# Other kinds for the late taps of a convolution, and another form for some VectorE products

## The chip, the cores and the metric

The kernel runs on one core of one Trainium2 chip. The core has TensorE for matmuls (PE in the profile, its weight loads are PEld), VectorE (DVE), ScalarE (ACT), GpSimd (POOL) and SyncE (SP), and 16 DMA engines that all queues share. Each engine works through its own instructions in the order of the program; semaphores hold an instruction until what it needs is done. The metric is the time of one execution on the device in microseconds (us), the median over several executions. Before the change it is 2298.85 us, from three runs between 2296.11 and 2299.28.

## The reference

A two-layer encoder works on a residual stream of 1024 positions by 1024 columns in float32. In each layer an attention with eight heads and a depthwise convolution run side by side on the same projection, and their joined outputs go through one matrix; then follows a gated feed-forward part. What matters here, cut from the reference:

```python
for l in range(DEPTH):
    h = _rmsnorm(x, g_mix[l])
    p = h @ w_in[l]
    ...                                                # q_nope, q_rope, k_nope, k_rope, v from p
    y_attn = _mla_attention(q_nope, q_rope, k_nope, k_rope, v)
    a, gt = jnp.split(p[..., o3:], 2, axis=-1)
    u = a * jax.nn.sigmoid(gt)
    u = _dwconv(u, w_dw_conv[l], b_dw_conv[l])         # 31 taps per channel, 512 channels
    u = jax.nn.silu(_layernorm(u, g_conv_ln[l], b_conv_ln[l]))
    x = x + jnp.concatenate([y_attn, u], axis=-1) @ w_o[l]
    ...                                                # gated feed-forward part
```

A tap of the convolution multiplies a shifted copy of `u` by one weight per channel and adds it to the sum. 31 taps on four tiles of 128 channels by 1024 positions make 124 products and additions for each layer.

## The kernel before

Every layer is projection, attention, output matrix and feed-forward part, one after the other on TensorE. Values for matmuls are split into a high and a low part (`hi` and `lo`, float32 rounded to TensorE's format and what is left), and a product is three matmuls: high by high, high by low, low by high.

**Attention** runs over 64 steps in a layer, 8 heads times 8 blocks of 128 queries. A step n issues, in program order for every engine: the product of probabilities and values for an earlier block (`values`, L1532, tile `o`), the transposes of the probabilities (`turn`, L1509, tile `t`, split by ACT at L1511 and VectorE at L1512), the scores of step n+2 (`scores`, L1480), the exponentials of step n+1 (`expo`, L1490 on ACT), and then whatever hangs in `agenda[n]`. Work beside attention is placed by this agenda: an entry sets the place in each engine's instruction order, not a time.

**What hangs in the agenda.** A finished half of a head's output is copied by ACT (L1537) and completed by VectorE (L1538) into `yt`; two heads share one `yt`. POOL multiplies pairs of heads by the reciprocal sums (L1558), ACT and POOL split them into `ys` high and low (L198, L200). For the next to last head the product is done by VectorE in two halves (L1556), in steps 60 and 61. In step 55 POOL issues the first four DMAs of the output matrix `wo`, which cast while they load (L836); from step 58 on ACT writes the negative of each arrived, rounded part into a second tile (L179), and a DMA from POOL adds the weight itself there (L180), which leaves the low part. In steps 60 to 62 POOL adds up the four convolution tiles (L1701), for the norm over channels.

**The taps.** The nearest 56 taps of the 124 are done by VectorE while TensorE projects (L1673, one fused multiply and add). Some more are done there by ACT and a DMA that adds. What is left, 50 taps in layer 0 and 48 in layer 1, are the late taps: the function `tap_late` (L1682 on) does each in one of three kinds, with its product in a tile `late` of its own:

- `act`: ACT multiplies in two halves (L1687), and a DMA issued by POOL adds the product to the sum (L1695, accumulating).
- `pool`: POOL multiplies (L1690), the same kind of DMA adds.
- `both`: POOL multiplies (L1690) and POOL adds (L1693).

The accumulating DMAs stand in POOL's queue. Before it adds to a tile of the sum, an addition of either sort waits for the addition before it to the same tile; the taps go round the four tiles (`conv` 0 to 3), which have different numbers of late taps left, and the last few all belong to `conv` 3. Which kind a tap has, and in which step it stands, is set by

```python
kinds = [LATE_KINDS[2 * i // len(late)][i % 5] for i in range(len(late))]
costs, taken = [LATE_COST[kind] for kind in kinds], set()
for i, (j, t) in enumerate(late):
    n, steps = int(SIDE_TIME * sum(costs[:i]) / sum(costs)), self.tap_late(l, j, t, u[j], conv[j], kinds[i])
```

so the first half of the taps follows the first tuple of `LATE_KINDS`, the second half the other, five in turn; and the 56 steps of `SIDE_TIME` are shared out in proportion to `LATE_COST` (1.1 for `act`, 3.5 for `pool`, 4.8 for `both`). A change of kind therefore moves the other taps too.

The tiles named here (`late`, `yt`, `rb`, `ys`, `conv`) come from one set of 31 equal buffers of 128 by 1024 floats; a new tile takes over a free buffer and waits for the last reader of the old one.

**Ahead of attention** VectorE subtracts the rounded parts of the queries from the queries: `query_rope` at L694 twice in a layer, `query` at L709 four times.

Of the kernel before, what the change touches and what calls it, by code (L numbers as in the profile page):

```python
# [9 lines left out]
F32 = mybir.dt.float32  # L10
F32R = mybir.dt.float32r
I32 = mybir.dt.int32
AF = mybir.ActivationFunctionType
ALU = mybir.AluOpType
# [48 lines left out]
LAST_MULT = (60, 61)  # L63
# [2 lines left out]
ROW_AT = {0: (6,), 1: (7,)}  # L66
E = mybir.EngineType
MANUAL = [E.PE, E.DVE, E.Activation, E.Pool]
LATE_KINDS = (("pool", "both", "act", "pool", "act"), ("both", "pool", "both", "pool", "both"))
LATE_COST = {"act": 1.1, "pool": 3.5, "both": 4.8}  # L70
NEAR_TAPS = (12, 14, 16, 14)
NEAR_ORDER = (0, 1, 2, 3)
# [43 lines left out]
class Encoder:  # L116
# [398 lines left out]
    def project(self, l, carry):  # L515
        nc, a = self.nc, self.a
# [160 lines left out]
        def query_rope(i):  # L677
            p = ps[f"u{i}"]
            c, s = self.blk(f"rc{l}_{i}"), self.blk(f"rs{l}_{i}")
            nc.vector.tensor_tensor(out=c, in0=p, in1=st["cos"], op=ALU.mult)  # L680
            nc.vector.tensor_tensor(out=s, in0=p, in1=st["sin"], op=ALU.mult)
            st["rope", i] = c, s
            yield 2.44, 0.0
            if i == 0:
                return
            (c1, s1), (c2, s2) = st.pop(("rope", 0)), st.pop(("rope", 1))
            nc.vector.tensor_tensor(out=c1, in0=c1, in1=s2, op=ALU.subtract)
            nc.vector.tensor_tensor(out=c2, in0=c2, in1=s1, op=ALU.add)
            his = [self.blk(f"qr{l}_{i}", F32R) for i in range(2)]
            for hi, o in zip(his, (c1, c2)):  # L690
                nc.scalar.copy(out=hi, in_=o)
            yield 2.5, 1.0
            for i, (hi, o) in enumerate(zip(his, (c1, c2))):
                nc.vector.tensor_tensor(out=o.bitcast(F32R), in0=o, in1=hi.bitcast(F32), op=ALU.subtract)  # L694
                sp = hi, o.bitcast(F32R)
                yield 1.25, 0.0
                for p in range(2):
                    for h in range(DIRECT):
                        self.move(heads[h][0][p][NOPE + i * HALF:NOPE + (i + 1) * HALF, :],
                                  sp[p][h * HALF:(h + 1) * HALF, :])  # L700
                spills.extend((qrd[p][i].rearrange("h d t -> (h d) t"), sp[p]) for p in range(2))

        def query(j):
            n = self.blk(f"qn{l}_{j}")
            nc.vector.tensor_tensor(out=n, in0=ps[f"n{j}"], in1=st["rq"], op=ALU.mult)
            hi = self.blk(f"qns{l}_{j}", F32R)
            nc.scalar.copy(out=hi, in_=n)
            yield 1.22, 1.5
            nc.vector.tensor_tensor(out=n.bitcast(F32R), in0=n, in1=hi.bitcast(F32), op=ALU.subtract)  # L709
            sp = hi, n.bitcast(F32R)  # L710
            for p in range(2):
                for e in range(DIRECT if j == 0 else 0):
                    self.move(heads[e][0][p][0:NOPE, :], sp[p][e * 64:(e + 1) * 64, :])
                spills.append((qd[p][2 * j:2 * j + 2].rearrange("h d t -> (h d) t"), sp[p]))
            while j and spills:
                self.move(*spills.pop(0))
            yield 1.25, 0.0
# [56 lines left out]
        for i in range(2):  # L774
            held = lambda: launch(query_rope(0), len(seq) - 6)
            add(f"u{i}", "u2", ranked("u2", i, QL, f"u{i}", cqs), lambda i=i: query_rope(1) if i else iter(()), held if i else norm)
        for j in range(4):
            add(f"n{j}", f"u{j // 2}", ranked(f"u{j // 2}", j % 2, QL, f"n{j}", cqs), lambda j=j: query(j))
# [670 lines left out]
    def attention(self, l, u, conv, away, spill, kvs, loaded, ahead, wo, begun):  # L1449
        nc = self.nc  # L1450
# [66 lines left out]
        def values(group, c, n):  # L1517
            h, gg = divmod(group, 2)
            st = state[h]
            e = h % 2  # L1520
            main, aux = slice(e * 64, e * 64 + 64), slice(64 - e * 64, 128 - e * 64)
            if c == 0:
                if gg == 0 and e == 0:
                    st["y"], st["rb"] = self.blk(f"yt{l}_{h}"), self.blk(f"rb{l}_{h}")
                elif gg == 0:
                    st["y"], st["rb"] = state[h - 1]["y"], state[h - 1]["rb"]
                st["po"] = self.bank(f"o{l}_{h}_{gg}")
            y, rb, po = st["y"], st["rb"], st["po"]
            pt = st["pt"].pop((c, gg))
            for s in range(2):  # L1530
                for i in range(2):
                    nc.tensor.matmul(po, v[2 * c + i][:, h // 2, e, :], pt[s][:, i, :],  # L1532
                                     start=(c == 0 and i == 0 and s == 0), stop=(c == 3 and i == 1 and s == 1))
            if c < 3:
                return
            qs = HALVES[gg]
            nc.scalar.copy(out=y[main, qs], in_=po[aux, :])  # L1537
            nc.vector.tensor_tensor(out=y[main, qs], in0=po[main, :], in1=y[main, qs], op=ALU.add)  # L1538
            if h < HEADS - 2 and gg:
                agenda[n + 1].append(lambda: sums(h, main, st, y, rb))  # L1540
            elif h == HEADS - 1:
                if gg:
                    divide(y[main, qs], main, gg)
                else:
                    agenda[n + 1].append(lambda: (divide(y[main, qs], main, gg), finish(last, y, 0)))

        def sums(h, main, st, y, rb):
            pr = self.bank(f"sr{l}_{h}", (8, 128))
            nc.tensor.transpose(pr, st["sums"], self.ident)
            rs = self.cp.tile([8, 128], F32, name=f"rs{l}_{h}", tag="rs", bufs=2)  # L1550
            nc.vector.reciprocal(out=rs, in_=pr)
            nc.sync.dma_start(out=sd[h].rearrange("(a b) -> a b", a=8), in_=rs)
            nc.sync.dma_start(out=rb[main, :], in_=sd[h:h + 1].partition_broadcast(64))
            if h == HEADS - 2:
                for c, cs in enumerate(HALVES):
                    agenda[LAST_MULT[c]].append(lambda cs=cs: nc.vector.tensor_tensor(out=y[main, cs], in0=y[main, cs], in1=rb[main, cs], op=ALU.mult))  # L1556
            elif h % 2:
                agenda[h * 8 + 10 + Y_DELAY].append(lambda: nc.gpsimd.tensor_tensor(out=y, in0=y, in1=rb, op=ALU.mult))  # L1558
                agenda[h * 8 + 10 + Y_DELAY + (Y_DELAY if h < 5 else Y_LAST)].append(
                    lambda: ys.append(self.split(y, f"ys{l}_{h}", on_pool=True)))  # L1560
# [31 lines left out]
        agenda = defaultdict(list)  # L1592
        late = [(j, away[j][i]) for i in range(max(map(len, away.values()))) for j in range(4) if i < len(away[j])]
# [4 lines that stand above are left out]
# [10 lines left out]
        last = HEADS - 1  # L1608
        state_y = lambda: state[last]["y"]
        agenda[56].append(lambda: sums(last - 1, slice(0, 64), state[last - 1], state[last - 1]["y"], state[last - 1]["rb"]))  # L1610
        agenda[60].append(lambda: [self.load_y(l, begun["x"], 0, k) for k in range(2)])
        for c, when in enumerate((60, 62)):
# [213 lines left out]
```

## Time and profile before

| | |
|---|---|
| median of three runs | 2298.85 us (2296.11 to 2299.28) |
| profiled execution, its own time | 2302.91 us |
| its span | 2301.1 us |
| mean granted TensorE clock | 0.996 |
| TensorE busy | 2275.6 us |
| VectorE, ScalarE, GpSimd busy | 1734.1, 1280.9, 812.5 us |
| late products on POOL (L1690) | 79, median 2.17 us |
| late additions on POOL (L1693) | 40, median 2.37 us |
| accumulating DMAs of late taps (L1695) | 58, of about 0.5 MB each, median 7.1 us from issue to landing |

The span runs from the first to the last instruction; 1.8 us of the execution's time lie around it. The attention of layer 0 lies between 203 and 431 us, that of layer 1 between 1349 and 1576 us. A row of a timeline gives start and duration in us, engine, line, operation, the tile written and the tiles read; a bracket at its end gives the time for which the engine was idle before it, and what ended that. Rows that follow one another and are alike are drawn together with their count. The duration of a DMA row is what the issue took on the engine, not the transfer. An engine's idle time costs nothing unless TensorE ends up waiting.

### The profile page before, as it was taken

The numbers are of one execution on the slowest core, as the hardware profiler recorded it, in microseconds if no ns is written. First come the engines' busy times: TensorE is split into PE (matmuls) and PEld (weight loads), VectorE is DVE, ScalarE is ACT, GpSimd is POOL, SyncE is SP. The second block draws the span as 40 slices with busy tenths as digits, with TensorE's granted clock in tenths as the row PEclk, the third lists the DMA queues.
The fourth block names the chain that finished last, engine by engine and source line by source line (L and its number), as shares of the span: only waits on it lengthen the run. The fifth ranks groups of instructions, "written<-read, shape, count | busy, mean of one in ns | idle before, by whom it ended". The sixth has DMA issues, their size and how long they took to land. (4 is left out here: it accounts for less than half of the span.)

```text
span 2301.1 us, 30485 instructions
## 1 busy us (share of the span) xinstructions
PE 2275.6 (99%) x10672; PEld 1887.9 (82%) x10672; DVE 1734.1 (75%) x2330; ACT 1280.9 (56%) x2034; POOL 812.5 (35%) x812
## 2 busy tenths in 40 slices
PE   9999999899999999999999999999999999999998
PEld 7888888688888888888888888888888888888887
DVE  6998878668867776776659888887697777768665
ACT  5355877545755555544533558774466555555443
POOL 1222798612333333001412337984323333320032
PEclk9999999999999999999999999999999999999999
DMA  6889974836899999944977999558559999988356
GB/s 184 164 181 270 196 154 93 227 102 168 192 259 292 283 288 246 299 145 121 218 156 152 192 269 201 129 124 206 173 123 226 272 299 282 290 218 309 101 130 158
DMA packets 196265, 465.36 MB, mean 202 GB/s; under 512 B 27040, under 2 KB 35344, under 8 KB 196112
## 3 DMA queue, kind: packets, MB, share of 16 engines
q0 software_dynamic: 100256, 212.10, 45.7%
q1 hardware_dynamic: 95280, 250.80, 32.8%
q8 instruction: 84, 1.38, 0.2%
q14 instruction: 69, 0.57, 0.1%
q10 hardware_dynamic: 576, 0.52, 0.1%
HBM read 309.28 MB, written 80.40 MB: 169 GB/s over the span
## 5 line engine op out<-in xcount | busy, mean ns | idle before, releaser
L1062 PE MATMUL p<-b,w 128*128 128x512 f32 x3552 | 806.9, 389 | 0.2 <-DVE zv L1011 0.2
L1062 PEld LDWEIGHTS p<-b,w 128*128 128x128 f32 x3552 | 666.3, 188 | 140.3 <-DVE w L1421 0.8
L1250 PE MATMUL pd<-ab,wd 128*128 128x512 f32 (+1 forms) x1920 | 422.3, 381 | 0.0
L1250 PEld LDWEIGHTS pd<-ab,wd 128*128 128x128 f32 x1920 | 350.7, 188 | 69.5 <-DVE ab L1421 0.4
L180 POOL DMA_DIRECT2D w<-wu x96 | 84.8, 890 | 364.4 <-ACT w L179 320.8
L1480 PE MATMUL s<-k,q 96*128 96x512 f32 x768 | 208.4, 406 | 0.0
L1512 DVE TENSOR_TENSOR pt<-t,pt 128x512 fp32r<-128x512 f32 x256 | 165.1, 686 | 53.6 <-ACT pt L1511 51.8
L1511 ACT CAST pt<-t 128x512 fp32r<-128x512 f32 x256 | 137.8, 589 | 66.3 <-PE t L1509 64.9
L1690 POOL TENSOR_TENSOR late<-gate,par 128x1018 f32<-128x1018 f32 (+12 forms) x79 | 166.7, 2110 | 18.8 <-issue 9.6
L1433 DVE SCALAR_TENSOR_TENSOR o<-zg,par,o 128x1023 f32<-128x1023 f32 x88 | 112.8, 1284 | 75.8 <-ACT o L1427 74.5
L180 POOL DMA_DIRECT2D w<-in_w_up x116 | 100.6, 867 | 195.4 <-ACT w L179 174.5
L1482 DVE TENSOR_REDUCE mx<-s 128x1 f32<-128x1024 f32 x128 | 156.0, 1219 | 0.3 <-PE s L1480 0.3
L1480 PEld LDWEIGHTS s<-k,q 96*128 96x128 f32 x768 | 135.5, 189 | 22.9
L1532 PE MATMUL o<-pt,v 128*128 128x512 f32 x512 | 141.6, 400 | 7.9 <-ACT pt L1511 7.9
L1490 ACT ACTIVATE p<-s,mx 128x1024 f32<-128x1024 f32 x128 | 144.5, 1129 | 3.6 <-DVE mx L1482 3.6
L1673 DVE SCALAR_TENSOR_TENSOR conv<-gate,par,conv 128x1009 f32<-128x1009 f32 (+7 forms) x112 | 142.3, 1275 | 3.6 <-ACT conv L574 1.0
L836 POOL DMA_DIRECT2D wd<-in_w_down x44 | 31.8, 723 | 309.8 <-PE pd L1250 169.4
L1509 PEld LDWEIGHTS t<-ident,p 128*128 128x128 f32 x1024 | 120.2, 141 | 22.1 <-DVE yt L1538 2.9
L1509 PE MATMUL t<-ident,p 128*128 128x128 f32 x1024 | 134.7, 274 | 3.2 <-DVE yt L1538 2.5
L179 ACT ACTIVATE w<-w 128x512 fp32r<-128x512 f32 x212 | 133.5, 630 | 3.0
L1419 ACT CAST ab<-ac 128x512 fp32r<-128x512 f32 x130 | 80.1, 617 | 98.1 <-DVE ac L1185 95.7
L1011 DVE TENSOR_TENSOR zg<-p,zg 128x512 f32<-128x512 f32 x88 | 60.6, 690 | 96.2 <-PE p L1062 89.5
(2113 smaller groups left out, 4142.1 us busy)
## 6 DMA issues: line engine op xcount, KB each, us to landing
w<-in_w_up POOLq DMA_DIRECT2D x232, 256.0 KB, 7.3
wu<-in_w_up SPq DMA_DIRECT2D x88, 512.0 KB, 6.0
w<-wu POOLq DMA_DIRECT2D x96, 256.0 KB, 5.7
sd<-in_w_down SPq DMA_DIRECT2D x44, 512.0 KB, 10.1
ws<-sd SPq DMA_DIRECT2D x44, 512.0 KB, 7.0
wd<-in_w_down POOLq DMA_DIRECT2D x88, 256.0 KB, 5.5
act<-v SPq DMA_DIRECT2D x36, 512.0 KB, 5.4
ac<-act SPq DMA_DIRECT2D x72, 256.0 KB, 6.0
```

Source lines behind the costliest of these rows:

```text
L180: self.nc.gpsimd.dma_start(out=lo, in_=src, accum_op=ALU.add)
L1062: nc.tensor.matmul(ps, w[p][:, k * 128:(k + 1) * 128], b[:, q], start=(i in (1, 5, 2) and k == 0 and t == 0), stop=(k == 3 and t == 2), sk ...
L1250: nc.tensor.matmul(ps[t, m][:, cs], w[i, j][p][:, m * 128:(m + 1) * 128], b[:, q, cs], start=(i in (1, 5, 2) and j == 0 and s == 0), stop= ...
L1480: nc.tensor.matmul(ps[:, cs], q[i][0:96, qs], k[j][0:96, cs], start=(s == 0), stop=(s == 2))
L1482: nc.vector.tensor_reduce(out=mx, in_=ps, op=ALU.max, axis=AX.X, negate=True)
L1490: nc.scalar.activation(out=p, in_=ps, func=AF.Exp, bias=mx, accum_out=st["sums"][:, qt:qt + 1])
L1509: nc.tensor.transpose(tp[:, i, qi * 128:(qi + 1) * 128], st["p"][2 * qp + qi][:, kt * 128:(kt + 1) * 128], self.ident)
L1511: nc.scalar.copy(out=hi, in_=tp)
L1512: nc.vector.tensor_tensor(out=lo, in0=tp, in1=hi.bitcast(F32), op=ALU.subtract)
L1532: nc.tensor.matmul(po, v[2 * c + i][:, h // 2, e, :], pt[s][:, i, :], start=(c == 0 and i == 0 and s == 0), stop=(c == 3 and i == 1 and s ...
L1673: self.nc.vector.scalar_tensor_tensor(out=y[:, lo:hi], in0=u[:, lo + s:hi + s], scalar=self.tap(l, j, t), in1=y[:, lo:hi], op0=ALU.mult, o ...
L1690: self.nc.gpsimd.tensor_tensor(out=p[:, lo:hi], in0=u[:, lo + s:hi + s], in1=self.tap(l, j, t).broadcast_to([128, hi - lo]), op=ALU.mult)
```

## The change

The second half of the late taps takes other kinds: of five, one is `both` and four are `pool`, where three were `both` and two `pool`. In layer 0 the late taps go from 40 POOL products, 20 POOL additions and 30 accumulating DMAs to 40, 10 and 40; in layer 1 from 39, 20 and 28 to 39, 10 and 38. As the kinds have different scheduled costs, the taps between the first and the last stand up to two steps later than before.

And four VectorE lines that read two operands from SBUF take another form: `tensor_tensor` becomes `scalar_tensor_tensor` with a first multiplication by 1.0. They are the subtractions of L694 (four in the whole kernel) and L709 (eight), and the products of L1556 (four). Nothing else changes.

```diff
-LATE_KINDS = (("pool", "both", "act", "pool", "act"), ("both", "pool", "both", "pool", "both"))
+LATE_KINDS = (("pool", "both", "act", "pool", "act"), ("pool", "both", "pool", "pool", "pool"))
...
             for i, (hi, o) in enumerate(zip(his, (c1, c2))):
-                nc.vector.tensor_tensor(out=o.bitcast(F32R), in0=o, in1=hi.bitcast(F32), op=ALU.subtract)
+                nc.vector.scalar_tensor_tensor(out=o.bitcast(F32R), in0=o, scalar=1.0, in1=hi.bitcast(F32), op0=ALU.mult, op1=ALU.subtract)
...
-            nc.vector.tensor_tensor(out=n.bitcast(F32R), in0=n, in1=hi.bitcast(F32), op=ALU.subtract)
+            nc.vector.scalar_tensor_tensor(out=n.bitcast(F32R), in0=n, scalar=1.0, in1=hi.bitcast(F32), op0=ALU.mult, op1=ALU.subtract)
...
             if h == HEADS - 2:
                 for c, cs in enumerate(HALVES):
-                    agenda[LAST_MULT[c]].append(lambda cs=cs: nc.vector.tensor_tensor(out=y[main, cs], in0=y[main, cs], in1=rb[main, cs], op=ALU.mult))
+                    agenda[LAST_MULT[c]].append(lambda cs=cs: nc.vector.scalar_tensor_tensor(out=y[main, cs], in0=y[main, cs], scalar=1.0, in1=rb[main, cs], op0=ALU.mult, op1=ALU.mult))
```

## The prediction

> **What bounds the kernel.** I read the page first, then PE's waits, then the rows of PE, ACT, DVE and POOL around each gap, in both layers.
>
> ```profile
> span 2301.1 us, 30485 instructions
> PE 2275.6 (99%) x10672; PEld 1887.9 (82%) x10672; DVE 1734.1 (75%) x2330; ACT 1280.9 (56%) x2034; POOL 812.5 (35%) x812
> PE o L1532 <- ACT pt L1511: 7.9, 2, 5.5
> ```
>
> TensorE is busy 99% of the span, and the diff touches none of its work. So a gain can only come out of PE's waits, a loss out of a new one. The largest waits in total stand on the last line: two, 7.9 us. PE's rows show where; the bracket ending a row is the idle time before it and its releaser.
>
> ```profile
> 339.25 1.46 PE L1532 MATMUL o<-pt,v 128*128 128x512 f32 x4 [2.40 <-ACT pt L1511]
> 402.28 1.63 PE L1480 MATMUL s<-k,q 96*128 96x512 f32 x6
> 409.40 2.08 PE L1532 MATMUL o<-pt,v 128*128 128x512 f32 x4 [5.48 <-ACT pt L1511]
> 412.83 1.95 PE L1480 MATMUL s<-k,q 96*128 96x512 f32 x6
> 426.02 1.47 PE L1509 MATMUL t<-ident,p 128*128 128x128 f32 x8 [2.46 <-DVE yt L1538]
> ...
> 1542.52 1.63 PE L1480 MATMUL s<-k,q 96*128 96x512 f32 x6
> 1545.72 1.63 PE L1480 MATMUL s<-k,q 96*128 96x512 f32 x6
> ```
>
> Three gaps, (a) at 339, (b) at 409 and (c) at 426, all in layer 0's attention. A step of attention takes 1545.72 - 1542.52 = 3.20 us; the one with (b) took 412.83 - 402.28 = 10.55, so (b) costs 7.35: 5.48 of idle time and 1.9 in which PE restarts slowly. With (a) and (c) at their idle time the three cost 2.40 + 7.35 + 2.46 = 12.2 us. ACT's rows name what stood behind the first two.
>
> ```profile
> 286.12 0.72 ACT L1687 ACTIVATE late<-gate,par 128x502 f32<-128x502 f32 x1
> 333.90 0.21 ACT L1490 ACTIVATION_READ_ACCUMULATOR p<-s,mx 128x1 f32 x1
> 338.00 0.58 ACT L1537 COPY yt<-o 64x512 f32<-64x512 f32 x1 [3.90 <-DMA conv<-late]
> 400.96 0.21 ACT L1490 ACTIVATION_READ_ACCUMULATOR p<-s,mx 128x1 f32 x1
> 407.50 0.63 ACT L179 ACTIVATE wo<-wo 128x512 fp32r<-128x512 f32 x1 [6.33 <-DMA wo<-in_w_o]
> ...
> 1499.44 1.05 ACT L198 CAST ys_3h<-yt 128x1024 fp32r<-128x1024 f32 x1
> 1544.48 0.64 ACT L179 ACTIVATE wo<-wo 128x512 fp32r<-128x512 f32 x1
> ```
>
> (a): ACT writes a head's yt into the memory of an earlier late product and waits until that product's DMA has read it. (b): ACT waits for the cast of wo. Both DMAs stand in POOL's queue, which in these stretches has no idle time but its own waits.
>
> ```profile
> 295.59 0.87 POOL L1695 DMA_DIRECT2D conv<-late  x1
> 318.89 2.41 POOL L200 TENSOR_TENSOR ys_1l<-yt,ys_1h 128x1024 fp32r<-128x1024 f32 x1
> 321.26 1.88 POOL L1690 TENSOR_TENSOR late<-gate,par 128x1016 f32<-128x1016 f32 x1
> 323.44 0.88 POOL L1695 DMA_DIRECT2D conv<-late  x1 [0.30 <-POOL late L1690]
> 324.04 2.19 POOL L1690 TENSOR_TENSOR late<-gate,par 128x1012 f32<-128x1012 f32 x1
> 328.64 1.87 POOL L1690 TENSOR_TENSOR late<-gate,par 128x1012 f32<-128x1012 f32 x1
> 330.81 0.88 POOL L1695 DMA_DIRECT2D conv<-late  x1 [0.30 <-POOL late L1690]
> 395.16 0.89 POOL L1695 DMA_DIRECT2D conv<-late  x1 [0.30 <-POOL late L1690]
> 400.87 2.36 POOL L1693 TENSOR_TENSOR conv<-conv,late 128x1009 f32<-128x1009 f32 x1 [2.91 <-DMA conv<-late]
> 403.17 2.21 POOL L836 DMA_DIRECT2D wo<-in_w_o  x4
> ...
> 1519.30 0.87 POOL L1695 DMA_DIRECT2D conv<-late  x1 [0.30 <-POOL late L1690]
> 1524.05 2.36 POOL L1693 TENSOR_TENSOR conv<-conv,late 128x1012 f32<-128x1012 f32 x1 [1.97 <-DMA conv<-late]
> 1539.77 2.22 POOL L836 DMA_DIRECT2D wo<-in_w_o  x4
> ```
>
> The DMA of (a) left at 330.81, when ACT was free 3.3 us later (333.90 + 0.21 = 334.11). The casts of (b) left at 403.17, behind the last tap, and reached ACT after 407.50 - 403.17 = 4.33 us; ACT had been free since 401.17. In layer 1 the casts left at 1539.77 and ACT took them at 1544.48 without a wait. POOL's lateness is what PE pays for in layer 0.
>
> **The change, part by part.**
>
> *Taps.* A tap with a DMA takes POOL from 321.26 to 324.04, 2.78 us after an addition, and 3.08 after another DMA (its product then takes 2.19 for 1.88); a tap with an addition takes 324.04 to 328.64, 4.60 after a DMA and about 4.28 after an addition. To test these prices on layer 0 before: from the last ACT tap's DMA (295.59, next instruction at +0.60) to the casts stand 10 DMA taps (27.8), 14 addition taps (ten at 4.60, four at 4.28: 63.1), four moved blocks of y such as L200 (321.26 - 318.89 = 2.37 each: 9.5) and some 7 us of waits: 107.4, and the trace has 403.17 - 296.19 = 107.0.
>
> After the change the same 24 taps are 5 with an addition and 19 with a DMA. The scheduled costs shrink too (177 to 164 in layer 0), so taps in between come up to two steps, 6.4 us, later: the last ACT product moves from 286.84 to about 293.2, still ahead of 295.59, so I keep that start. Up to the third DMA from the end: 5 x 4.60 + 6 x 2.78 + 10 x 3.08 + three blocks of 2.37 + a last product's 2.18 = 79.8, so it leaves at 376.0. The DMA that sets (a) free now has two additions' taps, two DMA taps at 2.78, two at 3.08, one block and a product ahead of it, 25.5 us: it leaves near 321.7 instead of 330.81, nine earlier against 3.9 needed: (a) goes.
>
> *The tail.* The last taps of both layers all add into the same quarter of the convolution, and each accumulating DMA there must wait until the one before has landed. Behind the waiting DMA POOL holds the casts of wo, a head's y (L1558, L200) and the totals (L1701); ACT's L179 waits for the casts. This is the new wait. Before, two additions waited there for one DMA each. What a landing takes:
>
> ```profile
> L1695 POOL DMA_DIRECT2D conv<-late x13: 869/886/1194, 289.5 to 395.2; - x13
> DMA to landing us min/median/max: 4.5/5.6/9.0
> DMA to landing us min/median/max: 4.6/7.9/13.9
> ```
>
> The second line is layer 0's second half, with the 13 of the first line; the third is layer 0's first half, where 18 such DMAs shared 87 us with the heads' loads. After the change 23 do so in the second half, so both are the bounds; I take 5.6, since in the tail only one accumulation is in flight (rows of before in that place: 1524.05 - 1519.30 = 4.75 and 400.87 - 395.16 = 5.71). Call it T. Layer 0's casts then leave at 376.0 + 2T + 0.6 = 387.8, where PE starts to lose only past 401.17 - 4.33 + 0.85 = 397.7 (ACT's 6.33 became 5.48 on PE): (b) goes, up to T = 10.5. Layer 1: ACT's L198 ends at 1500.49, then a block 2.37, taps 2.78 + 4.60 + 2.78 and a product 2.48 bring the first of three chained DMAs to 1515.5; with three landings, an addition 2.33 and a last tap 2.78 the casts leave at 1520.6 + 3T = 1537.4. Loss there begins at 1544.48 - 4.33 + 0.85 = 1541.0, so at T = 6.8. That is close.
>
> *VectorE.* Sixteen instructions change form.
>
> ```profile
> L709 DVE TENSOR_TENSOR qn<-qn,qns x8: 1216/1221/2918, 193.4 to 1347.8; 128x1024 fp32r<-128x1024 f32 x8
> L657 DVE SCALAR_TENSOR_TENSOR cqs_0l<-cq,par,cqs_0h x2: 1280/1282/1285, 145.7 to 1292.2; 128x1024 fp32r<-128x1024 f32 x2
> L1588 DVE SCALAR_TENSOR_TENSOR ys_7l<-yt,ys_7h x4: 692/693/1209, 430.2 to 1576.8; 128x512 fp32r<-128x512 f32 x4
> 416.05 3.55 DVE L1556 TENSOR_TENSOR yt<-yt,rb 64x512 f32<-64x512 f32 x1
> 421.85 3.39 DVE L1556 TENSOR_TENSOR yt<-yt,rb 64x512 f32<-64x512 f32 x1
> 1552.32 0.65 DVE L1556 TENSOR_TENSOR yt<-yt,rb 64x512 f32<-64x512 f32 x1
> 416.33 2.70 POOL L1701 TENSOR_TENSOR lns<-conv,conv 128x1024 f32<-128x1024 f32 x1
> ```
>
> The nearest price of the new form is 1282 - 1221 = +0.06 us at 1024 columns and nothing at 512: at most 12 x 0.06 = 0.7 us on VectorE (75% busy), of which I put 0.2 on the path; PE's projection matmuls cover it, and without that cover all 0.7 count. Below nothing: were the new form free of what held L1556 in (c), it alone would save 2.46. L1588 has that form and still took up to 1.21, so I count none.
>
> *Gap (c).* L1556 took 3.55 and 3.39 in layer 0 while POOL's L1701 ran beside it, and 0.65 in layer 1, where it began before that. With the casts early, layer 0's POOL is paced by ACT as in layer 1, and I let (c) go.
>
> Sum: -2.40 - 7.35 - 2.46 + 0.2 = -12.0 against the profiled execution's 2302.9, so 2290.9. That execution lies 4.1 above the median of the runs shown, 2298.85; whether its gaps are part of that isn't known. I take half: 2289.
>
> **The rivals.**
>
> Layer 1's tail (B): T between 6.8 and 10.5, as the first half's 7.9 speaks for and the chain's 4.75 against. At 7.9 the casts leave at 1544.3, 3.3 late; with the slow restart of 1.9 that is +5.2: 2294.
>
> The other side (C): the chained landings are long enough to make the casts late in both layers. Past T = 10.5 layer 1 alone loses 11 + 1.9, more than the 12 gained; at T = 12 its casts are 15.6 late (17.5 with the restart) and layer 0's 2.9, which leaves 2.6 of (b) saved and (a), (c): +9.6, about 2310. For it speaks the longest landing, 13.9; against it that nothing else accumulates in the tail.
>
> The lock moves (D): L1556 in layer 1 began 0.57 us ahead of POOL's L1701 there by the layers' common order; if phases shift, a 2.5 us gap stays or appears: about 2292.
>
> The change doesn't do it (E): yt's memory, wo's casts or POOL are held by something else after the reordering, and the gaps stay: 2296 to 2303.
>
> The new form is slow (F). Six subtractions per layer stand ahead of attention; were each twice as long, 6 x 1.22 = 7.3 us would come on the path in each layer: +14.6, so 2304. L1588's 693 ns at 512 columns, which at half rate would be near 1.22, speaks against it. [...]
>
> **How the numbers follow.** Forecast 0.48, B 0.18, C 0.13, D 0.11, E 0.06, F 0.04. A measurement of this kernel can tell about 0.2%, 4.6 us. Forecast, D and half of B are faster: 0.68. Same: the rest of B and E, 0.15. Slower: C, F and a little of E, 0.17. The likeliest case alone spans 2284 to 2294 (both readings of the 4.1 us, and (c)). With B, D and E the range is 2284 to 2303; C and F lie above.
>
> **What would show it.** Right: POOL's 20 additions L1693 in all instead of 40; layer 0's casts of wo near 388, layer 1's by 1541 (less whatever layer 0 gained); no idle time of ACT before L1537 or L179 in layer 0; PE waits of L1532 gone; L1556 below 1 us. Wrong: ACT waiting for wo in layer 1, accumulating DMAs landing above 7 us in the tail, L694 or L709 above 1.3 us, or L1556 again beside L1701.

## The result and the profile after

The changed kernel takes 2285.14 us (median, 2284.62 to 2287.63) against 2297.43 us (2295.17 to 2299.28) for the kernel before on the same chip: a ratio of 0.9949, 95% interval 0.9936 to 0.9961. It is faster by 12.3 us; 2289 was predicted, in a range of 2284 to 2303.

The profiled execution after took 2284.62 us. First the head of its page:

```profile
span 2282.9 us, 30513 instructions
PE 2270.1 (99%) x10672; PEld 1886.6 (83%) x10672; DVE 1727.1 (76%) x2330; ACT 1281.0 (56%) x2034; POOL 784.0 (34%) x812
```

Then PE's waits (total, times, longest):

```profile
PE rx_768s L285 <- DVE rx_768y L270: 1.9, 1, 1.9
PE warm L397 <- DVE ones L373: 1.1, 1, 1.1
...
PE t L1509 <- ACT p L1490: 0.7, 2, 0.4
```

The waits of L1532 for `pt` (7.9 us) and of L1509 for `yt` (2.5 us) are gone. What is left stands at the start and the end of the program; in attention no wait is longer than 0.4 us. POOL is busy 28.5 us less.

The rows of ACT that had waited, 3.90 us for a late tap's DMA and 6.33 us for `wo`:

```profile
333.55 0.58 ACT L1537 COPY yt<-o 64x512 f32<-64x512 f32 x1 [0.56 <-issue]
396.92 0.21 ACT L1490 ACTIVATION_READ_ACCUMULATOR p<-s,mx 128x1 f32 x1
397.01 0.64 ACT L179 ACTIVATE wo<-wo 128x512 fp32r<-128x512 f32 x1
```

POOL's timeline where the queue decides: the DMA that frees `yt`'s memory, the tail of layer 0 to its casts, and the tail of layer 1.

```profile
320.18 0.89 POOL L1695 DMA_DIRECT2D conv<-late  x1 [0.30 <-DMA k<-kd]
...
374.85 0.89 POOL L1695 DMA_DIRECT2D conv<-late  x1 [0.30 <-POOL late L1690]
379.92 0.89 POOL L1695 DMA_DIRECT2D conv<-late  x1 [2.27 <-DMA conv<-late]
385.76 0.89 POOL L1695 DMA_DIRECT2D conv<-late  x1 [3.05 <-DMA conv<-late]
386.36 2.47 POOL L836 DMA_DIRECT2D wo<-in_w_o  x4
...
1498.10 0.87 POOL L1695 DMA_DIRECT2D conv<-late  x1 [0.30 <-POOL late L1690]
1503.53 0.87 POOL L1695 DMA_DIRECT2D conv<-late  x1 [2.65 <-DMA conv<-late]
1509.88 0.87 POOL L1695 DMA_DIRECT2D conv<-late  x1 [3.56 <-DMA conv<-late]
1515.31 2.38 POOL L1693 TENSOR_TENSOR conv<-conv,late 128x1010 f32<-128x1010 f32 x1 [2.65 <-PE t L1509]
...
1520.43 2.44 POOL L836 DMA_DIRECT2D wo<-in_w_o  x4
```

Layer 0's casts leave at 386.36 instead of 403.17. The new wait is there too, in brackets: each accumulating DMA of the tail waits 2.3 to 3.6 us for the landing of the one before. (The addition at 1515.31 waits for the DMA of 1509.88, which landed at 1515.18; the view names another event of that moment.)

VectorE's rows: the products L1556 of layer 0, which had taken 3.55 and 3.39 us, and the subtractions.

```profile
404.86 0.65 DVE L1556 SCALAR_TENSOR_TENSOR yt<-yt,rb 64x512 f32<-64x512 f32 x1
407.77 0.92 DVE L1556 SCALAR_TENSOR_TENSOR yt<-yt,rb 64x512 f32<-64x512 f32 x1
L694 DVE SCALAR_TENSOR_TENSOR rc<-rc,qr x4: 1215/1218/1219, 190.0 to 1319.7; 128x1024 fp32r<-128x1024 f32 x4
```

The rest of the saving is in the clock. Stretches of the timeline before (duration, then each engine's busy time with its instructions, then granted clock, DMA share and GB/s), and in the second fence after:

```profile
405.00:410.00 5.00, 0.60 (x2) 0.50 (x2) 1.23 (x3) 2.45 (x5) 3.65 (x3) 0.67 0.88 279
410.00:415.00 5.00, 5.00 (x20) 4.20 (x19) 3.36 (x6) 4.73 (x9) 3.24 (x2) 0.65 0.65 104
...
428.00:431.00 3.00, 3.00 (x11) 2.42 (x10) 2.10 (x4) 0.73 (x2) 0.00 (x0) 0.57 0.31 102
```

```profile
405.00:410.00 5.00, 5.00 (x29) 4.23 (x28) 3.97 (x6) 4.35 (x9) 5.00 (x7) 1.00 0.43 62
```

Before, the granted clock fell after gap (b) and after gap (c): the slow restart. The 0.65 and 0.57 are means of these stretches; in finer ones the clock is 0.50 from 406.7 to 413.5 and from 427.2 to 430.6 us, and 1.00 in the rest of the attention. Set side by side matmul by matmul, the two profiled executions drift apart by 2.9 us over gap (a), 7.6 over (b) and 5.0 over (c), together 15.6 us. Their own times, 2302.91 and 2284.62, differ by 18.3: a further 1.1 us come from waits near the start that the change does not touch, and some 1.6 in small pieces behind the gaps. That is more than the 12.3 us between the medians. The kernel before may have smaller gaps in most executions, but only one was profiled, so this is not shown.

### The profile page after: what moved, and what is told of

It reads as the page before. It is cut to its first block, busy times and chain, and to the rows that moved or that the text cites. A ratio compares the mean times of both kernels' runs of the same rounds, so it can differ in the third digit from the quotient of the medians.

```text
span 2282.9 us, 30513 instructions
## 1 busy us (share of the span) xinstructions
PE 2270.1 (99%) x10672; PEld 1886.6 (83%) x10672; DVE 1727.1 (76%) x2330; ACT 1281.0 (56%) x2034; POOL 784.0 (34%) x812
## 4 chain that ended last, share of the span: by engine, by line
PE 95%; DVE 3%; DMA 1%; ACT 1%; issue 0%; POOL 0%; SPq 0%; DVEq 0%; ACTq 0%; POOLq 0%
PE p L1062 37%; PE pd L1250 18%; PE s L1480 8%; PE po L873 7%; PE o L1532 5%; PE t L1509 5%; PE pa L216 2%; PE pg L216 2%; PE pg L512 2%; DVE conv L1673 2%; PE pn L216 1%; PE pq L216 1%; PE pv L1461 1%; PE pkv L216 1%; PE pa L512 1%; PE pk L216 1%
## 5 line engine op out<-in xcount | busy, mean ns | idle before, releaser
L1690 POOL TENSOR_TENSOR late<-gate,par 128x1018 f32<-128x1018 f32 (+12 forms) x79 | 172.4, 2183 | 19.3 <-DVE qn L709 10.1
L1532 PE MATMUL o<-pt,v 128*128 128x512 f32 x512 | 140.3, 397 | 0.0
L836 POOL DMA_DIRECT2D wd<-in_w_down x44 | 32.7, 746 | 309.4 <-PE pd L1250 308.4
L179 ACT ACTIVATE w<-w 128x512 fp32r<-128x512 f32 x212 | 133.5, 630 | 3.0
L1509 PEld LDWEIGHTS t<-ident,p 128*128 128x128 f32 x1024 | 119.6, 140 | 18.5 <-ACT p L1490 1.2
L1509 PE MATMUL t<-ident,p 128*128 128x128 f32 x1024 | 133.3, 273 | 0.7 <-ACT p L1490 0.7
```

The costliest lines, as they stand in the source:

```text
L1509: nc.tensor.transpose(tp[:, i, qi * 128:(qi + 1) * 128], st["p"][2 * qp + qi][:, kt * 128:(kt + 1) * 128], self.ident)
L1690: self.nc.gpsimd.tensor_tensor(out=p[:, lo:hi], in0=u[:, lo + s:hi + s], in1=self.tap(l, j, t).broadcast_to([128, hi - lo]), op=ALU.mult)
```

## The experiments

The theory: PE paid for POOL's lateness, and shorter work in POOL's queue is the whole gain. Its rivals: the new form of VectorE's instructions, which might escape POOL; and the places of the taps, which moved with the costs.

**The new kinds alone, forms as before.**

```diff
-LATE_KINDS = (..., ("both", "pool", "both", "pool", "both"))
+LATE_KINDS = (..., ("pool", "both", "pool", "pool", "pool"))
```

> Theory (POOL's queue): the new kinds alone take all of the change's effect, about 12 us below the kernel before (ratio 0.9945 to 0.996); layer 0's casts of wo leave near 386 us, no PE wait of L1532, L1556 below 1 us though it is still a tensor_tensor. Rival (the new form of the VectorE instructions frees them from POOL): L1556 and with it gap (c), 2.5 to 5 us, come back, so at most 0.997.

Measured: 2285.41 us, ratio 0.9936 (0.9923 to 0.9949): all of the gain. VectorE's line for L1556, still in the old form:

```profile
L1556 DVE TENSOR_TENSOR yt<-yt,rb x4: 652/782/921, 405.4 to 1538.6; 64x512 f32<-64x512 f32 x4
```

Its casts left at 390.33, 4 us later than after the change, and PE still did not wait. The old form has the same short L1556, so gap (c) went with the new kinds.

**The new forms alone, kinds as before.**

```diff
-nc.vector.tensor_tensor(out=..., in0=o, in1=hi.bitcast(F32), op=ALU.subtract)
+nc.vector.scalar_tensor_tensor(out=..., in0=o, scalar=1.0, in1=hi.bitcast(F32), op0=ALU.mult, op1=ALU.subtract)
... (L694, L709 and L1556)
```

> Theory: the new form alone changes nothing, ratio 0.999 to 1.001; gaps (a), (b) and (c) are all there, and L1556 again takes about 3.5 us beside POOL's L1701; L694 and L709 at 1.22 us. Rival (the form frees VectorE): L1556 at 0.65 us and gap (c) gone, 2.5 to 5 us faster. Rival (the form is slow): L694 and L709 near 2.4 us and 10 us slower or more.

Measured: 2299.43 us, ratio 0.9997 (0.9988 to 1.0006). From its PE waits, and its lines of L1556 and L709:

```profile
PE o L1532 <- ACT pt L1511: 6.9, 2, 5.6
...
PE t L1509 <- DVE yt L1538: 1.0, 1, 1.0
```

```profile
L1556 DVE SCALAR_TENSOR_TENSOR yt<-yt,rb x4: 653/790/3158, 416.8 to 1552.8; 64x512 f32<-64x512 f32 x4
L709 DVE SCALAR_TENSOR_TENSOR qn<-qn,qns x8: 1216/1219/2926, 193.1 to 1345.3; 128x1024 fp32r<-128x1024 f32 x8
```

The gaps stay, (a) and (c) smaller in this execution (1.3 and 1.0 us), and the new form takes up to 3.16 and 2.93 us where POOL's two-operand work runs beside it. The form is neither slower nor freer.

**The places alone, and the kinds alone in the old places.** Two kernels that part the two effects of `LATE_KINDS`; `NEW` and `OLD` stand for the second tuple after and before the change, and the second kernel has them the other way round.

```diff
+placed = [(LATE_KINDS[0], NEW)[2 * i // len(late)][i % 5] for i in range(len(late))]
-costs, taken = [LATE_COST[kind] for kind in kinds], set()
+costs, taken = [LATE_COST[kind] for kind in placed], set()
```

> The kinds of before, but each tap in the step that the new costs would give it. Theory: POOL's work is as long as before, so the casts of wo leave near 403 us in layer 0 and the time stays within 3 us of before (ratio 0.9985 to 1.0015), if anything slower since some taps stand later. Rival (the moved places made the gain): 0.995.

> The new kinds with each tap in its step of before, forms as before. Theory: POOL's shorter work is what counts, so about 12 us below before (0.9945 to 0.996), as with the new places. Rival (places): no gain, ratio 1.0.

Measured: places alone 2298.11 us, ratio 0.9989 (0.9977 to 1.0002), with its casts at 405.56 and ACT's L179 idle for 8.54 us (gap (a) was not there in its profiled execution, (b) was longer, 7.7 us of PE's idle time); kinds in the old places 2288.51 us, ratio 0.9948 (0.9929 to 0.9966). So the kinds are what counts. The intervals of 2288.5 and of the 2285.4 above overlap, so the 3 us between them are not clear of the noise; a part of it in the profile is one PE wait of 2.0 us for a head's keys early in layer 0, which no profiled execution in the new places shows, nor that of the kernel before. Whether the places remove that wait was not tested further.

**The casts ahead of the last taps, everything else as before.**

```diff
-WO_AT = 55
+WO_AT = 50
```

> The kernel before with one edit: the first casts of wo stand in step 50 instead of 55, ahead of the last taps in POOL's queue; kinds and forms as before. Theory (what PE paid for in gap (b) is that the casts stand behind late taps): ACT's L179 finds wo there, gap (b) goes, 7 us; POOL's y block L1558 then ends near 405.6, 0.6 after ACT wants it, which ACT's slack covers; gap (a), which hangs on another tap, stays. So 6 to 10 us below before, ratio 0.9957 to 0.9975, short of the change's 0.994. Rival (POOL late as a whole: another row of its queue is late next): ACT waits for L1558 or a total instead, gain under 3 us.

Measured: 2290.43 us, ratio 0.9951 (0.9936 to 0.9966). ACT's next wait was the one foreseen, a little longer:

```profile
398.85 0.64 ACT L179 ACTIVATE wo<-wo 128x512 fp32r<-128x512 f32 x1
...
403.97 1.05 ACT L198 CAST ys_5h<-yt 128x1024 fp32r<-128x1024 f32 x1 [1.15 <-POOL yt L1558]
```

One moved row (in each layer) takes most of what the change takes: (b) and (c) both went, and PE waits 1.1 us in their place. The gain is above what was expected; in the profiled execution gap (a) wasn't there either, since its DMA left 1.4 us earlier than in the kernel before (329.45) and landed in 5.5 us instead of 7.1. The edit doesn't touch that DMA, so (a) depends on how a transfer falls.

**The new kinds in layer 0 alone.**

```diff
+table = (LATE_KINDS[0], NEW) if l == 0 else LATE_KINDS
-kinds = [LATE_KINDS[2 * i // len(late)][i % 5] for i in range(len(late))]
+kinds = [table[2 * i // len(late)][i % 5] for i in range(len(late))]
```

> The new kinds in layer 0 alone, layer 1 and the forms as before. Theory: layer 1 had no gap to lose, so the whole gain is there, ratio 0.993 to 0.9955. Rival (half of the gain comes from layer 1): 0.997.

Measured: 2287.76 us, ratio 0.9942 (0.9927 to 0.9957). The gain is layer 0's.

**Gap (c) brought back.** The new kinds in the old and in the new form, with POOL's totals one step earlier.

```diff
-TOTAL_TIME = 60
+TOTAL_TIME = 59
```

> New kinds, tensor_tensor forms, and POOL's totals L1701 one step earlier, so that POOL's subtraction L200 and L1701 run back to back over the places of both L1556. Theory (two-operand instructions of VectorE wait out such POOL work): L1556 takes 2 to 3.5 us each in both layers, PE waits for yt L1538 1 to 3 us in each, and the time is 2 to 9 us above the new kinds alone (2285.4). Rival (gap (c) came from the late casts in another way): L1556 at 0.65 to 0.92, no loss.

> The same with the changed forms. Theory (the form makes no difference): the same as with tensor_tensor within 1.5 us, L1556 2 to 3.5 us each. Rival (the new form is free of the wait): L1556 at 0.65 us and 2285.

Measured: 2299.37 us in the old form and 2298.83 us in the new, ratios 0.9994 (0.9983 to 1.0004) and 0.9994 (0.9985 to 1.0004): the change's gain is gone, 14 us, where 2 to 9 were expected. VectorE's and POOL's rows in layer 0 in the old form, a stretch behind them with its granted clock, and the new form's L1556:

```profile
406.27 5.88 DVE L1556 TENSOR_TENSOR yt<-yt,rb 64x512 f32<-64x512 f32 x1
405.63 2.73 POOL L200 TENSOR_TENSOR ys_5l<-yt,ys_5h 128x1024 fp32r<-128x1024 f32 x1
408.56 3.03 POOL L1701 TENSOR_TENSOR lns<-lns,conv 128x1024 f32<-128x1024 f32 x1
```

```profile
413.00:418.00 5.00, 4.58 (x17) 3.64 (x16) 4.97 (x4) 2.86 (x5) 4.02 (x5) 0.66 1.02 213
```

```profile
405.30 5.87 DVE L1556 SCALAR_TENSOR_TENSOR yt<-yt,rb 64x512 f32<-64x512 f32 x1
```

A product of 0.65 us waited out two POOL instructions with a DMA issue between them, until the second was over at 411.59, and ended 0.56 us later. The mechanism is the one of (c), and the form makes no difference; the size was taken too small, because the wait spans both instructions and because the granted clock falls after it (0.66 in the row of 413 to 418). Set side by side with the new kinds alone, the run in the old form falls behind by 6.7 us in layer 0 and 6.5 in layer 1, around these products, and hardly anywhere else.

**The tail made longer.** The change with the last late product repeated in place, four and eight times more.

```diff
-    self.nc.gpsimd.tensor_tensor(out=p[:, lo:hi], ...)
+    for _ in range(1 + extra):          # extra = 4 or 8 for the last late tap of a layer, else 0
+        self.nc.gpsimd.tensor_tensor(out=p[:, lo:hi], ...)
```

> The changed kernel with the last late product of each layer computed four times more into the same tile, so that the casts of wo leave about 7.5 us later (4 x 1.87) in layer 1 and 4.5 later in layer 0, where 3.05 us of waiting for a landing hide a part. Margins by the profile after: layer 0 397.13 - 4.33 + 0.85 - 386.36 = 7.3 us, layer 1 1527.14 - 4.33 + 0.85 - 1520.43 = 3.2. Theory (slack, then one for one, and a slow restart of 1.9): no PE wait in layer 0, 4.3 us in layer 1, 6 us above the change, about 2291. Rival (POOL's time in the tail counts from its first us): 12 us above. Rival (the casts have more slack than that): no loss.

> The same with eight repetitions: casts 15 us later in layer 1, 12 in layer 0. Theory: PE waits 11.8 us in layer 1 and 4.6 in layer 0, with two slow restarts 20 us above the change, about 2305, that is slower than the kernel before; L1701 meets L1556 again in the layers where the casts are late, which may add 2.5 us each. Rival (POOL's time counts from its first us): 27 us above. Rival (more slack): under 10.

Measured: 2303.11 us (ratio 1.002, 1.0002 to 1.0037) and 2316.21 us (1.0074, 1.0059 to 1.0089), 18 and 31 us above the change's 2285.14 (16 and 29 by the ratios) where 6 and 20 were expected. The margin was smaller than the theory had it, in both layers. With four repetitions, POOL's casts in layers 0 and 1, and ACT's wait behind each:

```profile
394.61 2.46 POOL L837 DMA_DIRECT2D wo<-in_w_o  x4
1534.47 2.44 POOL L837 DMA_DIRECT2D wo<-in_w_o  x4
...
402.00 0.63 ACT L180 ACTIVATE wo<-wo 128x512 fp32r<-128x512 f32 x1 [4.23 <-DMA wo<-in_w_o]
1540.37 0.63 ACT L180 ACTIVATE wo<-wo 128x512 fp32r<-128x512 f32 x1 [7.20 <-DMA wo<-in_w_o]
```

(This kernel's lines are one higher, L837 for L836.) From issue to ACT the casts took 7.39 and 5.90 us, not the 4.33 of before. Before, the last tap ended with an addition, and no accumulating DMA was under way when the casts left; after the change one leaves 0.6 us ahead of them. The landings of the first casts, before and after in layer 0 (the least value of each line is the first cast's):

```profile
DMA to landing us min/median/max: 4.3/5.0/5.2
DMA to landing us min/median/max: 5.5/6.2/6.6
```

Before, this is not a figure of idle DMA engines in layer 0: loads from another queue kept them busy (a DMA share of 0.96 between 402.0 and 403.1); in layer 1, where they were idle ahead of the casts, the first cast landed in 3.0 us. With four repetitions, in layer 0 the margin is then 7.3 - 3.1 = 4.2 us, and the casts were 8.25 later, 0.6 of it brought along from the start of the program: PE waited 3.38. On top come the falls of the clock (0.82 between 405 and 410 here, 0.51 between 1542 and 1547), by estimate about 2 us in layer 0 and some 4 in layer 1. Side by side with the change this run falls behind by 5.0 us in layer 0 and 10.9 in layer 1.

**DMAs alone in the second half.**

```diff
-LATE_KINDS = (..., ("pool", "both", "pool", "pool", "pool"))
+LATE_KINDS = (..., ("pool", "pool", "pool", "pool", "pool"))
```

> The second half of the late taps all with DMAs, no addition by POOL, forms as in the change. Theory: nothing is left to win in attention, and layer 1's tail becomes four chained landings; with the 5.4 to 6.4 us that they took after the change, its casts leave near 1502 + 4 x 5.9 + 0.6 = 1526 against a limit of 1523.7, so PE waits 2.5 us there and the time is 3 to 5 us above the change, about 2289. Rival (POOL is still what bounds): 2 us or more below the change. Rival (chained landings are covered): 2285.

Measured: 2300.2 us, ratio 0.9998 (0.9984 to 1.0012): one addition in five less, and by the median the whole gain is lost (the executions lie between 2290.0 and 2305.0, so some keep a part of it). POOL's tail and ACT's wait in layer 0, and ACT's in layer 1:

```profile
372.87 0.89 POOL L1695 DMA_DIRECT2D conv<-late  x1 [0.30 <-POOL late L1690]
380.71 0.89 POOL L1695 DMA_DIRECT2D conv<-late  x1 [5.04 <-DMA conv<-late]
386.84 0.89 POOL L1695 DMA_DIRECT2D conv<-late  x1 [3.34 <-DMA conv<-late]
392.98 0.89 POOL L1695 DMA_DIRECT2D conv<-late  x1 [3.34 <-issue]
393.59 2.46 POOL L836 DMA_DIRECT2D wo<-in_w_o  x4
...
401.44 0.63 ACT L179 ACTIVATE wo<-wo 128x512 fp32r<-128x512 f32 x1 [3.86 <-DMA wo<-in_w_o]
1539.21 0.63 ACT L179 ACTIVATE wo<-wo 128x512 fp32r<-128x512 f32 x1 [4.00 <-DMA wo<-in_w_o]
```

Casts late in both layers are the picture of the prediction's rival C, for the next step in the same direction, but not by its condition, landings past 10.5 us: from issue to the next issue the three chained DMAs took 7.8, 6.1 and 6.1 us, and the cast 7.85 us. Of the third interval the landing itself was 4.6 us; what held POOL for the other 1.6 the view does not name. Side by side with the change the run falls behind by some 7 us in each layer. Only layer 1 had been expected to lose.

**The same with the casts ahead of the last taps.** `WO_AT = 50` added to it, as a way round the tail.

> As the run with DMAs alone in the second half, with the first casts of wo in step 50, ahead of the last taps. Theory (what that run lost, 15 us against the change, it lost because the casts stood behind chained landings and shared the DMA engines with the last of them): no wait of ACT's L179 for wo in either layer, no PE wait of L1532, and the time is back at 2284 to 2288, ratio 0.993 to 0.996. Rival (twenty more accumulating DMAs load the DMA engines too much, wherever the casts stand): it stays above 2293.

Measured: 2297.99 us, ratio 0.9995 (0.9986 to 1.0004). The time is the rival's, the cause in the profile mostly another: L179 has its `wo`, but POOL stood still at the casts, and ACT at what was queued behind them.

```profile
381.42 1.71 POOL L836 DMA_DIRECT2D wo<-in_w_o  x3 [10.77 <-PE s L1480]
...
409.31 1.04 ACT L198 CAST ys_5h<-yt 128x1024 fp32r<-128x1024 f32 x1 [7.37 <-POOL yt L1558]
```

POOL reached the casts 10.77 us before PE's scores released the memory that they write to, and the tail behind them came later. One of the chained landings there also took 8.0 us; how much of the loss is due to it was not parted. With the old kinds POOL had reached the same place at 384.43, when the memory was free.

## Why the prediction was right, point by point

- *Where the gain is.* Three gaps in layer 0 on POOL's account, and hardly anything else: shown by the new kinds alone, by layer 0 alone, and by the profile after. The forecast was 12.0 us against the profiled execution; the medians differ by 12.3, but the two profiled executions by 18.3, of which the gaps are 15.6. So that 12.0 comes so near to 12.3 is in part luck: all three gaps were priced too low for the execution that they were read from.
- *The 4.1 us by which the profiled execution lay above the median.* I took half of it as lying outside the gaps. That the gaps of this execution sum to 15.6 us against 12.3 between the medians fits larger gaps than usual, which one trace cannot show. With the gaps at 15.6 and all of the 4.1 inside them the forecast would have been 2302.9 - 15.6 = 2287.3 instead of 2289: the two errors partly cancelled. Another 1.4 us of the miss is the median of before, which is 2297.43 over six executions.
- *POOL's queue.* The third DMA from the end was put at 376.0 and the casts at 387.8; they left at 374.85 and 386.36, with PE 1.1 us ahead since the start. Layer 1's casts, put at 1537.4, left at 1520.43, with PE 17.5 us ahead by then. In the tail, T was taken as 5.6; from each chained DMA's issue to the next row that had waited for it took 5.07, 5.84, 5.43, 6.35 and 5.43, on average 5.6. (The landings themselves took 4.5 to 5.8; half a microsecond passes from landing to the next issue, which the forecast did not count apart.)
- *Gap (b)'s margin: the step that was wrong.* The casts' 4.33 us came from a row with no accumulating DMA ahead of them in POOL's queue. In the 18 tails of the kept traces in which one left 0.6 us ahead, the first cast landed after 5.5 us (layer 0 after the change) to 7.8 (layer 0 with DMAs alone); in the 10 in which none had just left, after 3.0 (layer 1 before) to 4.9. Both are seen in single runs too: with the new kinds in layer 0 alone, 5.6 in layer 0 and 3.1 in layer 1. What makes the long ones longer was not tested. So both margins were at least 1.2 us smaller than the limits of T, 10.5 in layer 0 and 6.8 in layer 1, allowed, and the repetitions and the DMAs alone show how near the change lies to losing everything.
- *Gap (c).* Priced at its idle time, 2.46 us; with the clock's fall it was 5.0 in the profiled execution. That the casts' time decides it is shown by the new kinds alone and by the moved casts alone, and that POOL's two-operand work holds L1556 by the earlier totals.
- *Gap (a).* It went, by the row of 320.18 (predicted near 321.7). It is 1.3 us with the forms alone and not there with the places alone or the casts early, so it need not be in every execution of the kernel before.
- *The forms.* The +0.06 us was mis-sized: L694 and L709 take 1.218 us in the new form (medians after) and 1.218 and 1.221 in the old (before); the row I took has its scalar in memory, these have a constant, which may be the difference but was not tested. No run shows a median near the doubled time that rival F reckons with.
- *The restart.* The price of 1.9 us was read from one step. The rows of granted clock show what it is. At (b), idle for 5.48 us, the clock was 0.50 for 6.83 us, from the middle of the gap on; (c), idle for only 2.46, lowered it as well, to 0.50 for 3.41 us, while (a), idle for 2.40, left it at 1.00, so here the length of a single gap did not decide it. The trace before says more: in the attention, the changes of the granted clock lie whole multiples of 3.41 us apart (406.69, 413.52, 427.17, 430.58). Set marks every 3.41 us through these moments: (b) has 2.8 and 2.7 us of its idle time in two stretches between marks, (c) has 2.3 in one, and behind each of the three the clock was 0.50 up to the next mark; (a) is cut into 1.6 and 0.8, and the clock stayed at 1.00. No run moved a gap against the marks, so this is a reading of one trace, not a test.
- *A sum in rival C.* Its terms come to about +10 us, not +9.6; nothing hangs on it.

## What to carry to other kernels

A queue that two engines wait for is priced by the time at which its one decisive row leaves, not by its busy share: POOL was 35% busy, yet one row at the end of its full stretch cost 7 us, and moving that row alone took most of the gain. When additions become DMAs, count each wait for a landing in the chain (2.3 to 3.6 us each in the tail here), and take a transfer's latency from a row with the same transfers ahead of it in its queue (here 5.5 to 7.8 us against 3.0 to 4.9). Before going a step further in a direction that paid, work out the margin that is left: the next step here lost all of it.

## What the runs showed of the hardware

- VectorE's product L1556, 0.65 us at its shortest, waited for the end of POOL's two-operand work beside it, across L200 and L1701 in a row, and took 5.88 us in `tensor_tensor` and 5.87 in `scalar_tensor_tensor` form (the earlier totals, layer 0).
- The first of the four casting DMAs of `wo`, issued 0.6 us after an accumulating DMA of about 0.5 MB on the same queue, landed after 5.5 to 7.8 us (18 tails); with none just issued ahead of it, after 3.0 to 4.9 (10 tails).
- A gap of TensorE cost up to twice its length where the granted clock fell behind it: 5.0 us for (c), idle for 2.46, with 0.50 for 3.41 us behind it, and 5.0 for the 3.38 of four repetitions in layer 0, with 0.82 between 405 and 410; but 2.9 for (a), idle for 2.40, at 1.00.
